# A decoder layer's up projection with the activations stationary: 512 weight columns moving, the result turned in squares and by transfers, the down projection in two parts

## The chip, the cores and the metric

The kernel runs on one core of a Trainium2 chip. The metric is the device time of one launch in microseconds (us), the median of three runs. The core has a matrix engine (TensorE, PE in the profile, with its weight loads on a row PEld), VectorE (DVE), ScalarE (ACT), GpSimd (POOL) and SyncE (SP, which here only issues DMA transfers). Each engine works through its own queue of instructions in order; semaphores tie the queues together.

## The reference

One layer of a decoder, 256 tokens of 2048 features, all in float32. The token mixers come first (an mLSTM and a forgetting attention, then an output projection); the change is in what follows, the gated MLP with a causal convolution of width 3 along the tokens:

```python
h = rms_norm(x, ffn_norm_g[i])            # (256, 2048)
u = h @ w_up[i]                           # (2048, 2 * 5632)
a, g = jnp.split(u, 2, axis=-1)           # (256, 5632) each
a = causal_dwconv(a, conv_w[i], conv_b[i])   # three taps along the tokens, one set per feature
x = x + (jax.nn.gelu(a, approximate=False) * g) @ w_down[i]
gate = jax.nn.sigmoid(rms_norm(x, ple_norm_g[i]) @ w_ple_gate[i])
x = x + gate * (p[i].astype(x.dtype) @ w_ple_proj[i])
```

## The kernel before, in words

**Precision.** Every float32 operand of a large product is split into a rounded part `hi` (type float32r, which PE takes at full rate) and a remainder `lo`; three products, hi by hi, hi by lo and lo by hi, are added up in PSUM. For the activations the parts lie side by side: a tile `[128 features, k, 512]` holds 256 tokens of hi and behind them 256 tokens of lo.

**The stream of weight blocks.** All weights are read once, in blocks of 128 x 1024 numbers (512 KB: two chunks of 128 rows by 512 columns), by `run_stream` (L205). For each block SP issues the load into a buffer `raw` (L218; four buffers, so four blocks ahead), ACT copies it to `hi` (L231), VectorE subtracts to get `lo` (L233), three blocks ahead of PE and in four buffers each, and then the block's function issues its matmuls. After each block `pull` takes some steps out of `side`, a list of generators with other work. The planner of the framework orders each engine's queue from this program text and a simulated run, so the text gives priorities and not the exact order.

**Two ways to multiply a block.** `token_group` (L242) keeps 128 tokens of the activations stationary and moves 512 weight columns past them: three matmuls (L261 to L263) for each of 2 chunks and 2 halves of the tokens, 12 matmuls of 512 columns a block; the result has tokens on partitions. It is used by the output projection (`catT`), by the down projection (`uT`) and by the gate after it (`x3T`). `wide_group` (L295), which only the up projection uses (`x2T`), keeps 128 x 128 of the weights stationary and moves activations: for each chunk and each of four groups of 128 columns, one matmul of 512 (weight hi past the tokens' hi and lo, L311) and one of 256 (weight lo past the tokens' hi, L312), 16 matmuls a block; the result has features on partitions, with 256 columns to be added to the other 256.

**The MLP.** The up projection runs over 11 quarters `q` of 512 features (a "quarter" of 4 x 128), each with 8 blocks for `a` and 8 for `g`: 176 blocks, 2816 matmuls. `up_a` and `up_g` add the two halves of a bank (`merge`, L724 and L725), multiply by the tokens' norm factors, which lie along the free dimension (`rb`, made by four small PE matmuls in `rstd_rows`, L165), apply the three taps with the features' scalars on the partitions (L738, L741), the GELU (L745), and the product with `g` (L759); `split_T` (L139, L140) writes the parts of the product into `uT`, which holds all 44 chunks of features. After all quarters, the down projection runs over four groups `c` of 512 output columns, each over 44 chunks of `uT` (22 blocks); `resid` adds its result to `xs` (L691) and transposes the sum on PE for the gate. All of this is issued in this order, on the same four buffers and queues; in this stage no generator is left in `side` and no DMA other than the weight loads is issued.

Of the kernel before, what the change touches and what calls it, by code (L numbers as in the profile page):

```python
# [9 lines left out]
F32 = mybir.dt.float32  # L10
F32R = mybir.dt.float32r
# [4 lines left out]
P = 128  # L16
S = 256
# [14 lines left out]

BLK = 1024
RAW, PARTS = 4, 4
AHEAD_DMA, AHEAD_SPLIT = 4, 3
PAD = 112


# [1 line left out]
def layer_kernel(  # L40
# [161 lines left out]
            except StopIteration:  # L202
                side.remove(job)

    def run_stream(blocks, pulls, ramp=False):  # L205

        nb = len(blocks)
        raws, parts = {}, {}
        split = 0
        for i in range(-AHEAD_DMA, nb):  # L210
            j = i + AHEAD_DMA
            if j < nb:
                src, _, _, load = blocks[j]
                if load is not None:
                    load()
                kb, n = src.shape[1], src.shape[2]
                raws[j] = wp.tile([P, BLK], F32, tag="raw", name=f"raw{j}", bufs=RAW)
                nc.sync.dma_start(out=raws[j][:, : kb * n].rearrange("p (k n) -> p k n", k=kb), in_=src)  # L218

            ahead = min(AHEAD_SPLIT, 1 + i // 2) if ramp else AHEAD_SPLIT  # L220
            while i >= -1 and split < min(nb, i + ahead + 1):
                j, split = split, split + 1
                src, _, prep, _ = blocks[j]
                if prep is not None:
                    prep()
                kb, n = src.shape[1], src.shape[2]
                w = kb * n
                raw = raws.pop(j)
                hi = wp.tile([P, BLK], F32R, tag="hi", name=f"hi{j}", bufs=PARTS)
                lo = wp.tile([P, BLK], F32R, tag="lo", name=f"lo{j}", bufs=PARTS)  # L230
                act.copy(hi[:, :w], raw[:, :w])  # L231
                last["hi"] = traced()
                dve.tensor_sub(lo[:, :w], raw[:, :w], f32(hi[:, :w]))  # L233
                parts[j] = [v[:, :w].rearrange("p (k n) -> p k n", k=kb) for v in (hi, lo)]
            if i >= 0:
                blocks[i][1](*parts.pop(i))
                pull(pulls)

    def wsrc(w, k0, kb, c0, n):
        return w[0, k0 * P : (k0 + kb) * P, c0 : c0 + n].rearrange("(k p) n -> p k n", p=P)  # L240

    def token_group(w, korder, actT, c0, n, finish, tag="mm", prep=None, load=None):  # L242

        st = {}
        blocks = []
        kb = min(BLK // n, 2 * len(korder))
        starts = [(k0, kb) for k0 in korder[:: kb // 2]]
        if load is not None:
            starts = [(0, 1), (1, 1)] + starts[1:]
        for bi, (k0, kb) in enumerate(starts):  # L250
            def fn(hi, lo, bi=bi, k0=k0):
                if bi == 0:
                    st["b"] = [bank(tag, f"tg{t}") for t in range(NT)]
                for t in range(NT):
                    o = st["b"][t][:, :n]
                    for i in range(hi.shape[1]):
                        a = actT()[:, k0 + i, :]
                        ah, al = a[:, t * P : (t + 1) * P], a[:, 256 + t * P : 256 + (t + 1) * P]
                        first = bi == 0 and i == 0
                        last = bi == len(starts) - 1 and i == hi.shape[1] - 1  # L260
                        pe.matmul(o, ah, hi[:, i, :], start=first, stop=False)  # L261
                        pe.matmul(o, ah, lo[:, i, :], start=False, stop=False)  # L262
                        pe.matmul(o, al, hi[:, i, :], start=False, stop=last)  # L263
                    if bi == len(starts) - 1:
                        finish(t, st["b"][t])
            pair = k0 % 2 == 0
            blocks.append((wsrc(w, k0, kb, c0, n), fn, pair and prep and (lambda k0=k0: prep(k0)) or None,
                           pair and load and (lambda k0=k0: load(k0)) or None))
        return blocks

    def feature_group(w, c0, actT, finish):
# [4 lines left out]
        for k0 in range(0, KD, 2):  # L276
            def fn(hi, lo, k0=k0):
                if k0 == 0:
                    st["b"] = [bank("mm", f"fg{j}").rearrange("p (j s) -> p j s", j=2) for j in range(2)]
                for j in range(4):  # L280
# [8 lines left out]
                        pe.matmul(o, lo[:, i, cols], a[:, 0:256], start=False, stop=last)  # L289
                    if k0 == KD - 2 and j % 2 == 1:  # L290
                        finish(j // 2, st["b"][j // 2])
            blocks.append((wsrc(w, k0, 2, c0, 512), fn, None, None))
        return blocks

    def wide_group(w, c0, actT, finish, tag):  # L295


        st = {}
        blocks = []
        for k0 in range(0, KD, 2):  # L300
            def fn(hi, lo, k0=k0):
                if k0 == 0:
                    st["b"] = [bank(tag, f"wg{j}") for j in range(4)]
                for j in range(4):
                    o = st["b"][j]
                    cols = slice(j * P, (j + 1) * P)
                    for i in range(2):
                        a = actT()[:, k0 + i, :]
                        first = k0 == 0 and i == 0
                        last = k0 == KD - 2 and i == 1  # L310
                        pe.matmul(o, hi[:, i, cols], a, start=first, stop=False)  # L311
                        pe.matmul(o[:, 256:512], lo[:, i, cols], a[:, 0:256], start=False, stop=last)  # L312
                    if k0 == KD - 2:
                        finish(j, o)
            blocks.append((wsrc(w, k0, 2, c0, 512), fn, None, None))
        return blocks

# [396 lines left out]


    with tc.tile_pool(name="ffn", bufs=1) as fp:
        uT = fp.tile([P, KF, 512], F32R, name="uT")
        rstd2 = rstd_of(ssq2, "ffn")
        rb = rstd_rows(rstd2, fp)
        rb2 = rb.unsqueeze(1).broadcast_to([P, 2, S])  # L720
        gl = {}

        def merge(dst, b):
            act.copy(dst, b[:, 256:512])  # L724
            dve.tensor_add(dst, b[:, 0:256], dst)  # L725

        def up_a(q):
            st = {}

            def f(jj, b):  # L730
                pair, j = divmod(jj, 2)
                if j == 0:
                    st["a"] = fp.tile([P, 2, S], F32, tag="a", name="a", bufs=2)
                    st["c"] = gl[q, pair] = fp.tile([P, 2, S], F32, tag="gl", name="c", bufs=3)
                a, c, k = st["a"], st["c"], 4 * q + jj
                merge(a[:, j], b)
                dve.tensor_mul(a[:, j], a[:, j], rb)
                act.activation(c[:, j], a[:, j], AF.Identity, scale=cT[:, 88 + k : 89 + k],  # L738
                               bias=cT[:, 132 + k : 133 + k])
                for d in (1, 2):  # L740
                    dve.scalar_tensor_tensor(out=c[:, j, d:S], in0=a[:, j, 0 : S - d],  # L741
                                             scalar=cT[:, 88 - 44 * d + k : 89 - 44 * d + k],
                                             in1=c[:, j, d:S], op0=ALU.mult, op1=ALU.add)
                if j == 1:
                    act.activation(c, c, AF.Gelu)  # L745
                    dve.tensor_mul(c, c, rb2)
            return f

        def up_g(q):
            st = {}  # L750

            def f(jj, b):
                pair, j = divmod(jj, 2)
                if j == 0:
                    st["u"] = fp.tile([P, 2, S], F32, tag="a", name="u", bufs=2)
                u, k = st["u"], 4 * q + 2 * pair
                merge(u[:, j], b)
                if j == 1:
                    dve.tensor_mul(u, u, gl.pop((q, pair)))  # L759
                    split_T(uT[:, k : k + 2, :], u)  # L760
            return f

        blocks = []
        x2 = aT["cur"]
        for q in range(KF // 4):
            blocks.extend(wide_group(w_up, q * 512, lambda: x2, up_a(q), "mm"))
            blocks.extend(wide_group(w_up, FF + q * 512, lambda: x2, up_g(q), "aux"))
        ssq3 = sm.tile([P, NT, 4], F32, name="ssq3")
        x3T = {}

# [2 lines left out]
                x3T["t"] = new_aT("x3T")  # L773
            return x3T["t"]

        for c in range(4):
            blocks.extend(token_group(w_down, list(range(0, KF, 2)), lambda: uT, c * 512, 512,
                                      resid(c, ssq3, get_x3T, g_ple)))


        r3, pj = {}, {}

# [3 lines left out]
        def gate_done(c0, n, last):  # L786
            def f(t, b):
                if "r" not in r3:
                    r3["r"] = rstd_of(ssq3, "ple")
                sg = fp.tile([P, 2, S], F32, tag="gl", name="sg", bufs=3).rearrange("p a b -> p (a b)")[:, :n]  # L790
                w = n // 2 if last and t == NT - 1 else n
                for c in range(0, n, w):
                    sc = sg[:, c : c + w]
# [7 lines left out]
        for c0, n in ((0, 512), (512, 512), (1024, 512), (1536, 256), (1792, 256)):  # L801
            blocks.extend(token_group(w_ple_proj, [0], lambda: pT, c0, n, proj_done, tag="aux"))
            blocks.extend(token_group(w_ple_gate, all_k, get_x3T, c0, n, gate_done(c0, n, c0 == 1792)))
        run_stream(blocks, 0)


# [28 lines left out]
```

## Time and profile before

| | |
|---|---|
| median of three runs | 1297.15 us (1296.51 to 1297.23) |
| span of the profiled execution | 1294.4 us |
| time around that span | 2.75 us, the median less the span |
| PE, PEld | 1288.3 us and 1123.9 us busy, 7060 instructions each |
| DVE, ACT, POOL | 754.9, 648.1 and 18.0 us busy |
| DMA | 238.69 MB, 184 GB/s |

A page of the profile gives, for one execution, the busy time of each engine, a strip of 40 slices (a digit is the busy share in tenths), the DMA queues, the chain of work that ended last (followed back from the last instruction, with shares of the span by line), and the costliest groups of instructions: line, engine, operation, result <- sources, shapes, count, then busy time and mean duration, then the idle time of that engine just before them and what ended it. L311 is line 311 of the kernel. Matmuls overlap, so the duration of one is longer than the distance from one to the next.

### The profile page before, as it was taken

What the parts mean: (1) busy time and instruction counts of PE and PEld (TensorE: products, weight loads), DVE (VectorE), ACT (ScalarE), POOL (GpSimd) and SP (SyncE); (2) the same over time, 40 slices, a digit from 0 to 9 for tenths busy, and PEclk for the clock granted to TensorE, in tenths of its full rate; (3) what the DMA queues carried; (4) which work ended last, traced back from release to release, by engine and by line L of the source; (5) the groups of instructions that cost most, each with busy time, mean ns of one, the idle gap of its engine ahead of it and who ended that gap; (6) DMA issues with size and microseconds to landing.
All of it is one profiled execution on the core that took longest, in us unless ns stands there. A gap on an engine that the chain in (4) does not pass through costs nothing.

```text
span 1294.4 us, 18152 instructions
## 1 busy us (share of the span) xinstructions
PE 1288.3 (100%) x7060; PEld 1123.9 (87%) x7060; DVE 754.9 (58%) x1008; ACT 648.1 (50%) x964; POOL 18.0 (1%) x33
## 2 busy tenths in 40 slices
PE   9999999999999999999999999999999999999998
PEld 7899999988888888888888888888888888888888
DVE  6455566644565565766676576667654545455554
ACT  7655545435554464555455454545543434444443
POOL 2000000000000000000000000000000000000000
PEclk9999999999999999999999999999999999999999
DMA  8577855546665666666666666666656665656663
GB/s 293 152 188 187 224 151 138 163 137 176 179 184 184 186 179 192 182 189 184 186 188 184 191 182 193 179 192 183 189 186 195 190 192 186 195 190 192 204 203 107
DMA packets 132039, 238.69 MB, mean 184 GB/s; under 512 B 7945, under 2 KB 28017, under 8 KB 131953
## 3 DMA queue, kind: packets, MB, share of 16 engines
q1 hardware_dynamic: 131072, 237.07, 61.7%
q8 instruction: 55, 0.90, 0.3%
q10 hardware_dynamic: 657, 0.43, 0.1%
q0 software_dynamic: 224, 0.03, 0.1%
q14 instruction: 31, 0.25, 0.1%
HBM read 235.40 MB, written 2.10 MB: 183 GB/s over the span
## 4 chain that ended last, share of the span: by engine, by line
PE 99%; DMA 0%; SPq 0%; DVE 0%; ACT 0%; issue 0%; DVEq 0%
PE wg L311 26%; PE tg L262 17%; PE tg L263 17%; PE tg L261 17%; PE wg L312 13%; PE fg L287 2%; PE fg L289 2%; PE fg L288 2%; PE xT L151 1%; PE mob L604 0%; DMA xs<-in_x_dram 0%; PE msc L578 0%; PE qkp L502 0%; PE sc L518 0%; PE ob L543 0%; PE rowb L489 0%
## 5 line engine op out<-in xcount | busy, mean ns | idle before, releaser
L233 DVE TENSOR_TENSOR lo<-raw,hi 128x1024 fp32r<-128x1024 f32 (+2 forms) x462 | 546.6, 1184 | 481.2 <-ACT hi L231 478.7
L231 ACT CAST hi<-raw 128x1024 fp32r<-128x1024 f32 (+2 forms) x462 | 470.4, 1018 | 567.9 <-PE tg L263 297.7
L311 PE MATMUL wg<-x2T,hi 128*128 128x512 f32 x1408 | 497.5, 399 | 0.0
L312 PE MATMUL wg<-x2T,lo 128*128 128x256 f32 x1408 | 395.4, 281 | 0.0
L311 PEld LDWEIGHTS wg<-x2T,hi 128*128 128x128 f32 x1408 | 264.5, 188 | 65.8
L312 PEld LDWEIGHTS wg<-x2T,lo 128*128 128x128 f32 x1408 | 266.0, 189 | 0.1
L261 PE MATMUL tg<-hi,uT 128*128 128x512 f32 x352 | 137.2, 390 | 0.0
L262 PE MATMUL tg<-lo,uT 128*128 128x512 f32 x352 | 137.0, 389 | 0.0
L263 PE MATMUL tg<-hi,uT 128*128 128x512 f32 x352 | 137.0, 389 | 0.0
L261 PE MATMUL tg<-hi,hT 128*128 128x512 f32 (+1 forms) x384 | 135.7, 358 | 0.0
L262 PE MATMUL tg<-lo,hT 128*128 128x512 f32 (+1 forms) x384 | 135.6, 356 | 0.0
L263 PE MATMUL tg<-hi,hT 128*128 128x512 f32 (+1 forms) x384 | 135.0, 356 | 0.0
L262 PEld LDWEIGHTS tg<-lo,hT 128*128 128x128 f32 x384 | 72.2, 188 | 7.5
L263 PEld LDWEIGHTS tg<-hi,hT 128*128 128x128 f32 x384 | 71.8, 188 | 7.2
L263 PEld LDWEIGHTS tg<-hi,uT 128*128 128x128 f32 x352 | 66.1, 188 | 13.7
L262 PEld LDWEIGHTS tg<-lo,uT 128*128 128x128 f32 x352 | 66.1, 188 | 13.6
L261 PEld LDWEIGHTS tg<-hi,uT 128*128 128x128 f32 x352 | 66.1, 188 | 13.6
L261 PEld LDWEIGHTS tg<-hi,hT 128*128 128x128 f32 x384 | 71.8, 188 | 6.9
L287 PE MATMUL fg<-hT,hi 128*128 128x256 f32 x256 | 74.7, 292 | 0.0
L289 PE MATMUL fg<-hT,lo 128*128 128x256 f32 x256 | 73.1, 285 | 0.0
L288 PE MATMUL fg<-hT,hi 128*128 128x256 f32 x256 | 72.8, 284 | 0.0
L262 PE MATMUL tg<-lo,x3T 128*128 128x512 f32 (+1 forms) x160 | 55.5, 347 | 0.0
(212 smaller groups left out, 1186.7 us busy)
## 6 DMA issues: line engine op xcount, KB each, us to landing
raw<-in_w_up_dram SPq DMA_DIRECT2D x176, 512.0 KB, 3.8
raw<-in_w_down_dram SPq DMA_DIRECT2D x88, 512.0 KB, 4.6
raw<-in_w_in_dram SPq DMA_DIRECT2D x79, 512.0 KB, 3.7
raw<-in_w_in_dram SPq DMA_DIRECT2D x48, 344.0 KB, 3.4
raw<-in_w_out_dram SPq DMA_DIRECT2D x32, 512.0 KB, 3.9
raw<-in_w_ple_gate_dram SPq DMA_DIRECT2D x32, 512.0 KB, 4.1
xs<-in_x_dram SPq DMA_DIRECT2D x8, 256.0 KB, 7.0
raw<-in_w_ple_proj_dram SPq DMA_DIRECT2D x3, 512.0 KB, 3.8
```

Source lines behind the costliest of these rows:

```text
L151: pe.transpose(bk[:, t * P : (t + 1) * P], xs[:, t, k * P : (k + 1) * P], ident)
L231: act.copy(hi[:, :w], raw[:, :w])
L233: dve.tensor_sub(lo[:, :w], raw[:, :w], f32(hi[:, :w]))
L261: pe.matmul(o, ah, hi[:, i, :], start=first, stop=False)
L262: pe.matmul(o, ah, lo[:, i, :], start=False, stop=False)
L263: pe.matmul(o, al, hi[:, i, :], start=False, stop=last)
L287: pe.matmul(o, hi[:, i, cols], a[:, 0:256], start=first, stop=False)
L288: pe.matmul(o, hi[:, i, cols], a[:, 256:512], start=False, stop=False)
L289: pe.matmul(o, lo[:, i, cols], a[:, 0:256], start=False, stop=last)
L311: pe.matmul(o, hi[:, i, cols], a, start=first, stop=False)
L312: pe.matmul(o[:, 256:512], lo[:, i, cols], a[:, 0:256], start=False, stop=last)
```

## The change

The up projection goes over to `token_group`; `wide_group`, `merge`, `up_a`, `up_g` and the use of `rstd_rows` here are removed. Its result now has tokens on partitions, and the taps need features there. So `up_evac` brings each bank out of PSUM on ACT with the tokens' norm factor as a scalar, and VectorE turns it in squares of 32 x 32, into a tile `sq`. After the last bank of a quarter a generator `ffn_job` is put into `side`: SP issues 16 transfers inside SBUF, each from 32 partitions to 32 others, which bring the squares into place in `Y`; then the taps are applied inside pieces of 32 tokens, and GpSimd makes what crosses the edges of the pieces (`halo`, `E`); then GELU, product and `split_T`. The tile `uT` keeps 24 chunks instead of 44, so the down projection is cut: after six quarters 20 chunks are multiplied for all four `c` and added to `xs` (`part_sum`), then the other five quarters follow, then the remaining 24 chunks. `run_stream` gets four more `raw` buffers in the second pool, eight loads ahead, and pulls two steps a block.

```diff
-AHEAD_DMA, AHEAD_SPLIT = 4, 3
+AHEAD_SPLIT = 3
+RAW_FFN = 4
+QF = 24
...
-    def run_stream(blocks, pulls, ramp=False):
+    def run_stream(blocks, pulls, ramp=False, more=None):
...
+        ring = RAW + (RAW_FFN if more else 0)
+        for i in range(-ring, nb):
+            j = i + ring
...
+                if j % ring < RAW:
+                    raws[j] = wp.tile([P, BLK], F32, tag="raw", name=f"raw{j}", bufs=RAW)
+                else:
+                    raws[j] = more.tile([P, BLK], F32, tag="raw", name=f"raw{j}", bufs=RAW_FFN)
...
-    def token_group(w, korder, actT, c0, n, finish, tag="mm", prep=None, load=None):
+    def token_group(w, korder, actT, c0, n, finish, tag="mm", prep=None, load=None, slots=10 ** 6):
...
-                        a = actT()[:, k0 + i, :]
+                        a = actT()[:, (k0 + i) % slots, :]
...
-    def wide_group(w, c0, actT, finish, tag):
...
-        uT = fp.tile([P, KF, 512], F32R, name="uT")
+        uT = fp.tile([P, QF, 512], F32R, name="uT")
         rstd2 = rstd_of(ssq2, "ffn")
-        rb = rstd_rows(rstd2, fp)
...
+        halo = [fp.tile([P, 4, NT, 4, 2], F32, name=f"halo{i}") for i in range(2)]
+        for h in halo:
+            pool.memset(h, 0.0)
+        sq = {}
+
+        def up_evac(q, ag):
+            def f(t, b):
+                if ag == 0 and t == 0:
+                    sq[q] = fp.tile([P, 2, 4, NT, 4, 32], F32, tag="sq", name="sq")
+                z = fp.tile([P, 512], F32, tag="z", name="z", bufs=3)
+                act.activation(z, b, AF.Copy, scale=rstd2[:, t : t + 1])
+                dve.transpose(sq[q][:, ag, :, t].rearrange("p j f r -> p f j r"),
+                              z.rearrange("p (f j c) -> p f j c", f=4, j=4))
+                if ag == 1 and t == NT - 1:
+                    side.append(ffn_job(q))
+            return f
+
+        def ffn_job(q):
+
+            T = sq.pop(q)
+            Y = fp.tile([P, 2, 4, NT, 4, 32], F32, tag="Y", name="Y")
+            for i in range(4):
+                for j in range(4):
+                    nc.sync.dma_start(out=Y[32 * j : 32 * j + 32, :, i], in_=T[32 * i : 32 * i + 32, :, j])
+                    if j % 2 == 1:
+                        yield
+            yield
+            yield
+            a, g = Y[:, 0], Y[:, 1]
+            taps = [cT[:, 44 * w + 4 * q : 44 * w + 4 * q + 4] for w in range(4)]
+            c = fp.tile([P, 4, NT, 4, 32], F32, tag="c", name="c")
+            H = halo[q % 2]
+            E = fp.tile([P, 4, NT, 4, 2], F32, tag="E", name="E", bufs=2)
+            e1 = fp.tile([P, 8, 4], F32, tag="e1", name="e1", bufs=2)
+            Hm, Em = (v.rearrange("p i t f e -> p (i t) f e") for v in (H, E))
+            pool.tensor_copy(H[:, 1:4].rearrange("p i t f e -> p (i t f) e"),
+                             a[:, 0:3, :, :, 30:32].rearrange("p i t f e -> p (i t f) e"))
+            pool.tensor_copy(H[:, 0, 1], a[:, 3, 0, :, 30:32])
+            pool.tensor_tensor(out=Em, in0=Hm, in1=taps[0].unsqueeze(1).unsqueeze(3).broadcast_to([P, 8, 4, 2]),
+                               op=ALU.mult)
+            pool.tensor_tensor(out=e1, in0=Hm[..., 1], in1=taps[1].unsqueeze(1).broadcast_to([P, 8, 4]), op=ALU.mult)
+            pool.tensor_tensor(out=Em[..., 0], in0=Em[..., 0], in1=e1, op=ALU.add)
+            am, cm = (v.rearrange("p i t f r -> p (i t) f r") for v in (a, c))
+            for f in range(4):
+                act.activation(cm[:, :, f], am[:, :, f], AF.Identity, scale=taps[2][:, f : f + 1],
+                               bias=taps[3][:, f : f + 1])
                 for d in (1, 2):
+                    dve.scalar_tensor_tensor(out=cm[:, :, f, d:32], in0=am[:, :, f, 0 : 32 - d],
+                                             scalar=taps[2 - d][:, f : f + 1], in1=cm[:, :, f, d:32],
+                                             op0=ALU.mult, op1=ALU.add)
+                if f % 2 == 1:
+                    yield
+            edge = c[..., 0:2].rearrange("p i t f e -> p (i t f) e")
+            dve.tensor_add(edge, edge, E.rearrange("p i t f e -> p (i t f) e"))
+            cf = c.rearrange("p i t f r -> p (i t f r)")
+            act.activation(cf, cf, AF.Gelu)
+            yield
+            u = a.rearrange("p i t f r -> p (i t f r)").rearrange("p (f t i r) -> p f t i r", f=4, t=NT, i=4)
+            for f in range(4):
+                dve.tensor_mul(u[:, f], c[:, :, :, f].rearrange("p i t r -> p t i r"),
+                               g[:, :, :, f].rearrange("p i t r -> p t i r"))
+            yield
+            k = 4 * q % QF
+            split_T(uT[:, k : k + 4, :], u.rearrange("p f t i r -> p f (t i r)"))
+            yield
...
+        def part_sum(c):
+            def f(t, b):
+                xc = xs[:, t, c * 512 : (c + 1) * 512]
+                dve.tensor_add(xc, b, xc)
+            return f
+
+        blocks = []
+        x2 = aT["cur"]
+
+        def up(q):
+            for ag in range(2):
+                blocks.extend(token_group(w_up, all_k, lambda: x2, ag * FF + q * 512, 512, up_evac(q, ag),
+                                          tag=("mm", "aux")[ag]))
+
+        def down(k0, k1, finish):
+            for c in range(4):
+                grp = token_group(w_down, list(range(k0, k1, 2)), lambda: uT, c * 512, 512, finish(c), slots=QF)
+                if c == 0:
+                    src, fn, _, _ = grp[-2]
+                    grp[-2] = (src, lambda hi, lo, fn=fn: (pull(10 ** 6), fn(hi, lo)), None, None)
+                blocks.extend(grp)
+
+        for q in range(6):
+            up(q)
+        down(0, 20, part_sum)
+        for q in range(6, KF // 4):
+            up(q)
+        down(20, KF, lambda c: resid(c, ssq3, get_x3T, g_ple))
...
-                sg = fp.tile([P, 2, S], F32, tag="gl", name="sg", bufs=3).rearrange("p a b -> p (a b)")[:, :n]
+                sg = fp.tile([P, 512], F32, tag="z", name="sg", bufs=3)[:, :n]
...
-        run_stream(blocks, 0)
+        run_stream(blocks, 2, more=fp)
```

More of the change, by code (lines that the diff above doesn't have):

```diff
@@ L209, in run_stream @@
         split = 0
-        for i in range(-AHEAD_DMA, nb):
-            j = i + AHEAD_DMA
+        ring = RAW + (RAW_FFN if more else 0)
+        for i in range(-ring, nb):
+            j = i + ring
             if j < nb:
@@ L216, in run_stream @@
                 kb, n = src.shape[1], src.shape[2]
-                raws[j] = wp.tile([P, BLK], F32, tag="raw", name=f"raw{j}", bufs=RAW)
+                if j % ring < RAW:
+                    raws[j] = wp.tile([P, BLK], F32, tag="raw", name=f"raw{j}", bufs=RAW)
+                else:
+                    raws[j] = more.tile([P, BLK], F32, tag="raw", name=f"raw{j}", bufs=RAW_FFN)
                 nc.sync.dma_start(out=raws[j][:, : kb * n].rearrange("p (k n) -> p k n", k=kb), in_=src)
@@ L291, in fn @@
                         finish(j // 2, st["b"][j // 2])
-            blocks.append((wsrc(w, k0, 2, c0, 512), fn, None, None))
-        return blocks
-    def wide_group(w, c0, actT, finish, tag):
[L298 to L314, printed above, removed]
             blocks.append((wsrc(w, k0, 2, c0, 512), fn, None, None))
@@ L716, in layer_kernel @@
     with tc.tile_pool(name="ffn", bufs=1) as fp:
-        uT = fp.tile([P, KF, 512], F32R, name="uT")
+        uT = fp.tile([P, QF, 512], F32R, name="uT")
         rstd2 = rstd_of(ssq2, "ffn")
-        rb = rstd_rows(rstd2, fp)
[L720 to L739, printed above, removed]
-                for d in (1, 2):
[L741 to L764, printed above, removed]
@@ L765, in layer_kernel @@
-        for q in range(KF // 4):
-            blocks.extend(wide_group(w_up, q * 512, lambda: x2, up_a(q), "mm"))
-            blocks.extend(wide_group(w_up, FF + q * 512, lambda: x2, up_g(q), "aux"))
+        halo = [fp.tile([P, 4, NT, 4, 2], F32, name=f"halo{i}") for i in range(2)]
[13 more added lines that the diff above has]
+            return f
@@ L774, in get_x3T @@
             return x3T["t"]
-        for c in range(4):
-            blocks.extend(token_group(w_down, list(range(0, KF, 2)), lambda: uT, c * 512, 512,
-                                      resid(c, ssq3, get_x3T, g_ple)))
+        def part_sum(c):
[22 more added lines that the diff above has]
+        down(20, KF, lambda c: resid(c, ssq3, get_x3T, g_ple))
         r3, pj = {}, {}
```

## Prediction

> **What bounds the kernel now.** I read the page first: the totals, the clock strip and the chain that ended last.
>
> ```profile
> span 1294.4 us, 18152 instructions
> ...
> PE 1288.3 (100%) x7060; PEld 1123.9 (87%) x7060; DVE 754.9 (58%) x1008; ACT 648.1 (50%) x964; POOL 18.0 (1%) x33
> ...
> PEclk9999999999999999999999999999999999999999
> ...
> PE 99%; DMA 0%; SPq 0%; DVE 0%; ACT 0%; issue 0%; DVEq 0%
> PE wg L311 26%; PE tg L262 17%; PE tg L263 17%; PE tg L261 17%; PE wg L312 13%; PE fg L287 2%; PE fg L289 2%; PE fg L288 2%; PE xT L151 1%; PE mob L604 0%; DMA xs<-in_x_dram 0%; PE msc L578 0%; PE qkp L502 0%; PE sc L518 0%; PE ob L543 0%; PE rowb L489 0%
> ```
>
> PE is busy in 100% of the span, the granted clock is full in every slice, and the chain is PE for 99%. So a change of this kernel is worth what it changes in PE's own time, plus any wait that it makes PE take. The up projection's two lines (L311, L312) carry 39% of the chain. The next view is the tile `wg`, which the up projection fills, with its matmuls and those who wait for them.
>
> ```profile
> L311 PE MATMUL wg<-x2T,hi x1408: 389/398/478, 449.0 to 947.4; 128*128 128x512 f32 x176
> ...
> L312 PE MATMUL wg<-x2T,lo x1408: 277/281/365, 449.3 to 947.6; 128*128 128x256 f32 x176
> ...
>   ACT hi L231: 204.0, 153
> ```
>
> The last row says that ACT's `hi` copy waits 204 us for these matmuls, while PE has no wait in this list: the splitting of weights runs ahead and is held back by PE, not the other way round. The windows view of most of the stage says the same by engine (columns: PE, PEld, DVE, ACT and POOL busy with counts, clock, DMA share, GB/s).
>
> ```profile
> 498.80:947.60 448.80, 448.80 (x2542) 389.19 (x2541) 297.49 (x416) 234.00 (x317) 0.00 (x0) 1.00 0.64 186
> ```
>
> PE is busy for all 448.80 us, DVE for 297.49 (66%), ACT for 234.00 (52%), DMA for 0.64 of it. There is no PE wait to remove; only the time per matmul can move.
>
> **The price per matmul, before and after.** L311 and L312 form 1408 pairs. The chain in order of time shows what else PE did inside these stages: transposes, in groups of eight.
>
> ```profile
> by line: PE wg L311 25.5%; PE tg L262 16.7%; PE tg L263 16.7%; PE tg L261 16.7%; PE wg L312 12.9%; PE fg L287 2.4%; PE fg L289 2.4%; PE fg L288 2.4%; PE xT L151 0.8%; PE mob L604 0.4%; DMA xs<-in_x_dram 0.3%; PE msc L578 0.3%; PE qkp L502 0
> ...
> 453.07 0.87 PE xT L151 x8
> 1012.55 0.87 PE xT L151 x8
> 1073.28 0.87 PE xT L151 x8
> 1134.01 0.87 PE xT L151 x8
> ```
>
> ```profile
> L165 PE MATMUL rstdb<-dg,ones x8: 270/273/275, 36.3 to 462.8; 128*128 128x128 f32 x8
> ```
>
> One transposing group (0.87 us, 0.109 us a matmul) lies in the up stage, and half of the eight `rstdb` matmuls, 0.4 us at the same 0.109. From the first to the last start of L311 are 498.4 us; less 1.3 that is 497.1 us for 1407 distances, 353.3 ns for a pair, 497.5 us for 1408 pairs. A pair moves 512 and 256 columns. What 512 columns cost in `token_group` form is shown by the down projection, which has the same instructions and shapes that the up projection is to get.
>
> ```profile
> L261 PE MATMUL tg<-hi,uT x352: 389/389/476, 947.8 to 1189.1; 128*128 128x512 f32 x176
> ...
> L263 PE MATMUL tg<-hi,uT x352: 389/389/393, 948.2 to 1189.6; 128*128 128x512 f32 x176
> ```
>
> From the first to the last start of L261 are 241.3 us, less three transposing groups in between (1012.55 to 1134.01) 238.7 us, for 351 x 3 = 1053 matmuls: 226.7 ns each. After the change there are 22 groups x 8 blocks x 12 = 2112 matmuls of 512 columns. That is the same number of columns, 1408 x 768 = 2112 x 512 = 1,081,344, in 704 fewer matmuls. So the new stage takes 2112 x 0.2267 = 478.8 us, 18.7 us less. A third form supports it: the mixers' `feature_group` moves 256 columns only.
>
> ```profile
> core 0: us, PE busy (x) PEld busy (x) DVE busy (x) ACT busy (x) POOL busy (x), PEclk, DMA share, GB/s
> 146.00:166.00 20.00, 20.00 (x168) 19.81 (x168) 12.08 (x23) 8.62 (x14) 0.00 (x0) 1.00 0.74 206
> ```
>
> Some 167 matmuls in 20.00 us are 120 ns each. From 120 for 256 and 226.7 for 512 follow 0.417 ns a column and 13 ns a matmul. 704 matmuls fewer at 13 ns are 9.4 us, half of the gain; the other half is that a pair takes 353.3 ns and not the 346.7 that its two lengths give alone. I have no cause for these 6.6 ns, but they belong to the alternation of the two lengths, which goes away.
>
> The Trainium skill (page "TensorE: Matmul & The Clock Gate", section "Back-to-back issue gap") gives a warm gap of the columns at 2.4 GHz plus 2.5 ns. By that the fixed part is small, the gain would be an estimated 704 x 2.5 ns = 1.8 us, and the change would hardly be worth measuring. The trace disagrees with this 2.5 ns here: 226.7 ns stands where the page's rule gives 215.8.
>
> **What else changes on PE.** The four `rstdb` matmuls go: 0.4 us less. The down projection stays at 88 blocks and 1056 matmuls; cut in two it has eight bank pairs rather than four, which changes no matmul. The gate at the end keeps its blocks.
>
> **What is added beside PE.** The terms of one quarter go by these rows (line, engine, operation; then busy time and mean ns).
>
> ```profile
> L738 ACT ACTIVATE c<-a,cT 128x256 f32<-128x256 f32 x44 | 24.1, 596 | 6.4 <-DVE a L737 6.4
> L724 ACT COPY a<-wg 128x256 f32<-128x256 f32 x44 | 16.2, 368 | 6.0 <-PE wg L312 6.0
> ...
> L745 ACT ACTIVATE c<-c 128x512 f32<-128x512 f32 x22 | 13.8, 627 | 0.3 <-DVE c L741 0.3
> ...
> L653 ACT ACTIVATE mv<-tg,rstd_mix 128x512 f32<-128x512 f32 x4 | 2.8, 690 | 1.9 <-PE tg L263 1.9
> ```
>
> ```profile
> L741 DVE SCALAR_TENSOR_TENSOR c<-a,cT,c 128x254 f32<-128x254 f32 x44 | 20.1, 478 | 0.0
> ...
> L725 DVE TENSOR_TENSOR a<-wg,a 128x256 f32<-128x256 f32 x44 | 16.5, 417 | 0.0
> ...
> L691 DVE TENSOR_TENSOR xs<-tg,xs 128x512 f32<-128x512 f32 x16 | 10.2, 682 | 0.0
> ```
>
> None of this can gain time, since PE waits for none of it now; the question is whether it stays hidden. ACT loses eight copies of 0.368 and gets four from PSUM with a scalar (0.69 each, L653); the taps (4 x 0.596, L738) and GELU (two of 0.627, now one of twice the length) stay: no more than before. VectorE loses 8 x 0.417 (L725) and all products with the norm factors, keeps the taps (8 x 0.478, L741), and gets four turns. The trace has no turn in squares. From below I set 0.417, a 128x256 operation with half the elements; from above four such, one for each 128 features, 1.7 us. I take 0.68, that of the 128x512 addition in L691, which reads and writes as many elements. The dearest case is 6.7 us a quarter; VectorE is idle in 34% of a quarter's 45.3 us (498.6 / 11), 15 us, so it is hidden in all of them, and up to some 3.8 us a turn. The eight `part_sum` additions (0.68 each) come once, beside PE.
>
> GpSimd gets five operations a quarter, on at most 64 numbers a partition. The trace has one of its kind only:
>
> ```profile
> L175 POOL TENSOR_TENSOR r_fk<-rs_v,neghalf 128x16 f32<-128x16 f32 x1 | 2.9, 2912 | 31.6 <-DVE rs_v L174 31.6
> ...
> L175 POOL TENSOR_TENSOR rstd_ffn<-rs_v,neghalf 128x2 f32<-128x2 f32 x1 | 0.7, 696 | 124.6 <-DVE rs_v L174 124.6
> ```
>
> These powers of 2 and 16 numbers bound the five at 3.5 and 14.5 us. I take 3.5: a copy, a product and a sum are no power. VectorE's edge addition waits for them.
>
> SP gets 16 transfers of 64 KB a quarter. The rows for its issue and the landing:
>
> ```profile
> L218 SPq DMA_DIRECT2D raw<-in_w_up_dram x176: 367/368/368, 431.6 to 927.9; - x176
> ...
> L218 SPq DMA_DIRECT2D raw<-in_w_ple_gate_dram x32: 367/368/739, 1176.0 to 1270.0; - x32
> ...
> DMA to landing us min/median/max: 2.4/3.9/7.2
> ```
>
> ```profile
> q1 hardware_dynamic: 131072, 237.07, 61.7%
> ```
>
> Issuing is 0.37 us whatever the size, so 16 more are 5.9 us a quarter beside 16 loads' 5.9. On the DMA engines, the first queue moved 131072 packets in 61.7% of 1294.4 us on 16 engines, 97 ns a packet. A quarter's 1 MB is 1024 pieces of 1 KB: by bytes 3.5 us, by packets 6.2 us of all engines, so DMA goes from 0.64 to at most 0.64 x 45.3 / 43.5 + 6.2 / 43.5 = 0.81. It stays under full.
>
> **The wait that the change adds.** In text order, ACT's taps stand behind the `hi` copy of the block eight after the quarter's last, and ahead of the copy of the ninth. If they wait for a transfer, so does that copy, and then VectorE and PE. How much room is there?
>
> ```profile
> 600.16 1.05 ACT L231 CAST hi<-raw 128x1024 fp32r<-128x1024 f32 x1 [1.74 <-PE wg L311]
> ...
> 601.24 1.22 DVE L233 TENSOR_TENSOR lo<-raw,hi 128x1024 fp32r<-128x1024 f32 x1 [1.56 <-ACT hi L231]
> ...
> 602.98 1.05 ACT L231 CAST hi<-raw 128x1024 fp32r<-128x1024 f32 x1 [1.77 <-PE wg L311]
> ```
>
> A `hi` copy starts when a block is through on PE, one every 2.8 us (2.72 after the change, 12 x 0.2267), and serves the block three later. Count from E, the end of the quarter's last block. Evacuation, turn and a split in front of them: the squares are ready by E + 3.7 (0.69 + 0.68 + 1.05 + 1.22; 1 us more if a turn takes 1.7). SP then issues 16 transfers and three loads, 19 x 0.367 = 7.0 us, and the last lands 3.9 us after its issue: E + 14.6. The copy of the ninth block may start at E + 13.6 (five blocks on), must be done with the subtraction by E + 21.8, so start by E + 19.5; the taps' four operations come before it, 2.4 us. So the transfers have until E + 17.1: 2.5 us to spare, and no time on PE. The edge addition stands before the subtraction of the tenth block, which must be through by E + 24.5: GpSimd has 8.7 us from the landing and takes 3.5. While SP waits for the squares, loads behind it wait too; with eight buffers they have some eight blocks (22 us) from issue to use and need 3.9, so that costs nothing. `uT` slots that are written again belong to chunks whose part of the down projection is long through. The last quarter's job has ten blocks (27 us) until its chunks are needed, and ends after about seven.
>
> **The sum.** 1294.4 - 18.7 - 0.4 = 1275.3 us of span; with the 2.75 us around it, which is the median 1297.15 less the span, **1278.0 us**.
>
> **Rivals.** *First, the transfers come late (slower).* The place is ACT's taps, L738's successor, in each quarter. Beyond E + 17.1 every microsecond stops PE once a quarter: 11 us. At 1.7 us late the gain is gone. For it: 2.5 us to spare is little, 7.2 us is the longest landing in the rows, and the trace has no transfer inside SBUF. At 7.2 instead of 3.9 PE would lose 0.8 x 11 = 9 us: 1287. If issuing cost 0.74 us (the longest row of L218) the last would land at E + 21.7, 4.6 late, 51 us: 1329. GpSimd at 14.5 us would be 5.8 late, 64 us: 1342. Against it: the longest issue is one of 32, a power is no copy, and the planner may bring `hi` copies ahead of waiting taps. *Second, the form brings nothing.* If in this stage time goes by columns alone, 353.3 / 768 = 0.460 ns each, 2112 x 512 of them take 497.4 us again and only `rstdb` is saved: 1296.7. If 512 columns keep what L311 has on the chain, 25.5% of 1294.4 over 1408 or 234.4 ns, the stage takes 495.1 us: 1294.3. Against it: the down projection's 226.7 has `hi` and `lo` moving just so, with the same splitting beside it. A cost of 2.5 ns a matmul, as the Trainium skill has it ("TensorE: Matmul & The Clock Gate", "Back-to-back issue gap"), would put the result near here, at an estimated 1294.9. *Third, small waits,* 0.2 to 1 us a quarter, from queues that the planner fills for times that differ from the chip's: 1281 to 1289.
>
> **Chances.** Forecast 0.72 (1275.5 to 1281; the lower end is a matmul of 225.5 ns, 0.5% less, 2.5 us in all). Third 0.12. First 0.10: 0.02 still faster, 0.01 same, 0.07 slower. Second 0.06: 0.01 faster, 0.05 same. 0.2% is 2.6 us, about what a measurement of this kernel can tell from no change. So faster by more than that 0.72 + 0.12 + 0.02 + 0.01 = 0.87, same 0.01 + 0.05 = 0.06, slower 0.07. The range goes to 1288, which takes in the forecast and nearly all of the third; the dear bounds of the first (1329, 1342) stay outside, with 0.18 in all.
>
> **What would show it.** Right: L261 to L263 with `x2T`, 704 of each, 226 to 227 ns apart; the stages up and down together (now 498.8 + 242) near 721 us with PE busy throughout; ACT's `hi` still waiting for PE; the turns near 0.7 us; the transfers landing in about 4 us. Wrong: PE rows with waits on ACT or DVE once a quarter some nine blocks after its end, ACT waiting on the DMA of `Y` for over 2 us, or a distance near 235 ns.

## The result and the profile after

The changed kernel takes **1278.34 us** (four runs, 1277.32 to 1279.7) against 1297.19 before (four runs): a ratio of 0.9853 with a 95% interval of 0.9839 to 0.9866, some 19 us less. The forecast was 1278.0. The profiled execution's span went from 1294.4 to 1275.4; its whole time is 1277.32, so 1.9 us lie around the span.

The page of the changed kernel, with the same lines as before:

```profile
span 1275.4 us, 16936 instructions
...
PE 1269.8 (100%) x6352; PEld 1088.8 (85%) x6352; DVE 732.3 (57%) x925; ACT 641.9 (50%) x898; POOL 33.2 (3%) x90
...
PEclk9999999999999999999999999999999999999999
...
PE 99%; DMA 0%; SPq 0%; DVE 0%; ACT 0%; issue 0%; DVEq 0%
PE tg L268 29%; PE tg L269 29%; PE tg L267 29%; PE fg L293 2%; PE fg L295 2%; PE fg L294 2%; PE xT L153 1%; PE mob L587 0%; DMA xs<-in_x_dram 0%; PE msc L561 0%; PE qkp L485 0%; PE sc L501 0%; PE ob L526 0%; PE rowb L472 0%; PE pt L520 0%; PE msc L564 0%
```

PE is still busy throughout, the clock is full, the chain is still PE. Only the lines in it are others: L267 to L269, the three matmuls of `token_group`, take what L311 and L312 had. The up projection's share of them, in the tile view of `x2T` (count, duration min/median/max, first and last start; then a waiter with total and times):

```profile
L267 PE MATMUL tg<-hi,x2T x704: 389/389/476, 449.2 to 1036.9; 128*128 128x512 f32 x176
...
L269 PE MATMUL tg<-hi,x2T x704: 389/389/393, 449.6 to 1037.4; 128*128 128x512 f32 x176
...
  ACT hi L237: 182.7, 114
```

And what the same matmuls do for the down projection, whose rows now straddle the second part of the up projection:

```profile
L267 PE MATMUL tg<-hi,uT x352: 389/389/476, 711.2 to 1170.1; 128*128 128x512 f32 x176
...
L269 PE MATMUL tg<-hi,uT x352: 389/389/393, 711.6 to 1170.6; 128*128 128x512 f32 x176
```

From the first start of L267 with `x2T` (449.2) to the first with `uT` (711.2) are 262.0 us; less one transposing group of 0.87, 261.1 us for six quarters of 192 matmuls: 226.7 ns each, as forecast. From the stage's start to the last down matmul (1170.6, and its 0.23) are 721.6 us; before, these two projections took 740.8 (449.0 to 1189.6, and 0.23). The 19.2 us between them are the whole change of the span, 19.0. ACT's `hi` copy still waits for PE; PE waits for nothing in these stages. The windows view of most of the first part:

```profile
498.80:709.00 210.20, 210.20 (x929) 174.07 (x928) 133.30 (x166) 112.54 (x127) 6.31 (x25) 1.00 0.67 219
```

The work that was added, in the tile views of `Y` and `sq` (SPq is SP's issue of a transfer):

```profile
L725 SPq DMA_DIRECT2D Y<-sq x176: 585/595/1703, 495.2 to 1049.2; - x176
...
  ACT c L746: 17.8, 11
...
DMA to landing us min/median/max: 2.0/2.0/3.7
```

```profile
L713 DVE STREAM_TRANSPOSE sq<-z x44: 701/705/712, 471.5 to 1038.5; 128x512 f32<-128x512 f32 x44
```

A turn takes 0.705 us, an issue 0.595, a landing 2.0. The end of the second quarter in order of time, ACT, VectorE and SP (start, duration, engine, line; in brackets the idle time before and what ended it):

```profile
537.30 0.69 ACT L712 ACTIVATE z<-tg,rstd_ffn 128x512 f32<-128x512 f32 x1 [0.67 <-PE tg L269]
...
538.03 0.71 DVE L713 STREAM_TRANSPOSE sq<-z 128x512 f32<-128x512 f32 x1 [0.51 <-ACT z L712]
...
538.80 10.71 SPq L725 DMA_DIRECT2D Y<-sq  x16
...
550.99 2.08 ACT L746 ACTIVATE c<-Y,cT 128x256 f32<-128x256 f32 x4 [1.75 <-DMA Y<-sq]
...
552.97 1.99 ACT L237 CAST hi<-raw 128x1024 fp32r<-128x1024 f32 x2
```

The quarter's last bank is through at 537.3. The 16 transfers are issued from 538.80 in one go, 10.71 us, and the taps wait for the last of them 1.75 us, until 550.99. That is 13.7 us behind the quarter's end, with the next `hi` copy at 15.7; it would have stopped PE from 19.5 on.

### The profile page after: what moved, and what is told of

Read it like the earlier page. It is cut to its first block, busy times and chain, and to the rows that moved or that the text cites. A ratio compares the mean times of both kernels' runs of the same rounds, so it can differ in the third digit from the quotient of the medians.

```text
span 1275.4 us, 16936 instructions
## 1 busy us (share of the span) xinstructions
PE 1269.8 (100%) x6352; PEld 1088.8 (85%) x6352; DVE 732.3 (57%) x925; ACT 641.9 (50%) x898; POOL 33.2 (3%) x90
## 4 chain that ended last, share of the span: by engine, by line
PE 99%; DMA 0%; SPq 0%; DVE 0%; ACT 0%; issue 0%; DVEq 0%
PE tg L268 29%; PE tg L269 29%; PE tg L267 29%; PE fg L293 2%; PE fg L295 2%; PE fg L294 2%; PE xT L153 1%; PE mob L587 0%; DMA xs<-in_x_dram 0%; PE msc L561 0%; PE qkp L485 0%; PE sc L501 0%; PE ob L526 0%; PE rowb L472 0%; PE pt L520 0%; PE msc L564 0%
## 5 line engine op out<-in xcount | busy, mean ns | idle before, releaser
L269 PE MATMUL tg<-hi,x2T 128*128 128x512 f32 x704 | 273.9, 389 | 0.0
L268 PE MATMUL tg<-lo,x2T 128*128 128x512 f32 x704 | 273.9, 389 | 0.0
L267 PE MATMUL tg<-hi,x2T 128*128 128x512 f32 x704 | 271.0, 389 | 0.0
L267 PEld LDWEIGHTS tg<-hi,x2T 128*128 128x128 f32 x704 | 132.1, 188 | 27.5
L268 PEld LDWEIGHTS tg<-lo,x2T 128*128 128x128 f32 x704 | 132.1, 188 | 27.4
L269 PEld LDWEIGHTS tg<-hi,x2T 128*128 128x128 f32 x704 | 132.1, 188 | 27.4
L267 PE MATMUL tg<-hi,uT 128*128 128x512 f32 x352 | 136.9, 390 | 0.0
L269 PE MATMUL tg<-hi,uT 128*128 128x512 f32 x352 | 136.8, 389 | 0.0
L267 PE MATMUL tg<-hi,hT 128*128 128x512 f32 (+1 forms) x384 | 135.7, 358 | 0.0
L269 PE MATMUL tg<-hi,hT 128*128 128x512 f32 (+1 forms) x384 | 135.0, 356 | 0.0
L269 PEld LDWEIGHTS tg<-hi,hT 128*128 128x128 f32 x384 | 71.8, 188 | 7.2
L269 PEld LDWEIGHTS tg<-hi,uT 128*128 128x128 f32 x352 | 66.1, 188 | 13.8
L268 PEld LDWEIGHTS tg<-lo,uT 128*128 128x128 f32 x352 | 66.1, 188 | 13.7
L267 PEld LDWEIGHTS tg<-hi,hT 128*128 128x128 f32 x384 | 71.8, 188 | 6.9
L267 PEld LDWEIGHTS tg<-hi,uT 128*128 128x128 f32 x352 | 66.1, 188 | 13.5
L293 PE MATMUL fg<-hT,hi 128*128 128x256 f32 x256 | 74.7, 292 | 0.0
```

The source lines that it names most:

```text
L293: pe.matmul(o, hi[:, i, cols], a[:, 0:256], start=first, stop=False)
```

## The experiments

All ratios are against the kernel before, timed beside each on the same chip.

**The form of the matmuls.** *Half width:* the changed kernel, each up matmul cut in two.

```diff
-                        pe.matmul(o, ah, hi[:, i, :], start=first, stop=False)
...
+                        w = cut or n
+                        for c in range(0, n, w):
+                            pe.matmul(o[:, c : c + w], ah, hi[:, i, c : c + w], start=first and c == 0, stop=False)
...
+                                          tag=("mm", "aux")[ag], cut=256))
```

> The changed kernel, with each matmul of the up projection cut in two of 256 columns: 4224 instead of 2112, same columns, same data path. The theory of 13 ns for every matmul (120 ns at 256) expects 4224 x 0.120 = 506.9 us instead of 478.8, 28 us more, about 1306. A rival with 2.5 ns a matmul expects 5 us more, 1284; columns alone expect 1278.

Measured 1307.29 us, ratio 1.0078 (1.0064 to 1.0092). That is 29 us over the changed kernel, for the same columns and the same data path, with 2112 matmuls more: 13.7 ns each, besides their columns. In the trace the halves start 120 ns apart. The Trainium skill ("TensorE: Matmul & The Clock Gate", "Back-to-back issue gap") has 2.5 ns for it; that would have been an estimated 5 us. The runs decide for 13, for this type of operand.

The 13 ns were fitted through two lengths, and the half-width run adds none, so a third one is worth reading: from 60 to 140 us the kernel before has nothing on PE but matmuls of 344 columns in `token_group` form. Its windows view there (PE alone):

```profile
60.00:140.00 80.00, 80.00 (x512) 1.00 0.72 191
```

511 distances in 80 us are 156.6 ns each; 0.417 ns x 344 columns and 13.3 ns are 156.7. So the three lengths lie on one line: a price by the column and a fixed price for each matmul. What inside PE takes the 13 ns is not shown by any run.

*Lengths grouped:* the kernel before, in each block first the eight long, then the eight short matmuls.

```diff
                 for j in range(4):
-                    o = st["b"][j]
...
+                        pe.matmul(st["b"][j], hi[:, i, cols], a, start=k0 == 0 and i == 0, stop=False)
+                for j in range(4):
...
                         pe.matmul(o[:, 256:512], lo[:, i, cols], a[:, 0:256], start=False, stop=last)
```

> The kernel before, with the sixteen matmuls of an up block put in another order: first the eight of 512 columns, then the eight of 256. Nothing else moves. The theory says that a pair's 353.3 ns are 226.7 + 120 plus 6.6 ns for the alternation of lengths: the stage shrinks by 1408 x 6.6 ns less the one change of length that is left in each half block, about 9 us, to 1288. The rival, that a column costs 0.460 ns in this stage in any order, expects 1297 as before.

Measured 1292.56, ratio 0.9960 (0.9946 to 0.9973): 5 us less, between the two (1288 and 1297). The chain in order of time of that kernel (L308 the long ones, L315 the short ones):

```profile
600.90 0.95 PE wg L315 x8
601.85 1.84 PE wg L308 x8
```

Eight long ones take 1.84 us, eight short ones 0.95, 2.79 us a block, where eight pairs took 2.83 and the plain sum of the lengths is 2.77. The starts in the trace show where the rest sits: behind the short ones the first five long ones take 228 to 236 ns, the last three 226 or 227. So a change of length costs some 20 ns a block here, and grouping saves only a part. This left the 6.6 ns a pair without a cause; the next run gave a lead by accident.

**The cut of the down projection.** *Down split only:* the kernel before, with nothing of the change but the two parts.

```diff
...
+        def down(k0, k1, finish):
+            for c in range(4):
+                blocks.extend(token_group(w_down, list(range(k0, k1, 2)), lambda: uT, c * 512, 512, finish(c)))
+
+        for q in range(6):
+            up(q)
+        down(0, 20, part_sum)
+        for q in range(6, KF // 4):
+            up(q)
+        down(20, KF, lambda c: resid(c, ssq3, get_x3T, g_ple))
```

> The kernel before, with only the down projection cut in two parts (20 chunks after six quarters, 24 at the end, eight part sums on VectorE); up projection, buffers and full uT as before. The theory puts this part at nothing: 1297.2 within 1 us. A rival in which the cut brings waits at its borders would show some microseconds more.

Measured 1292.61, ratio 0.9962 (0.9950 to 0.9975): 4.9 us *less*, where both theories had nothing or more. The windows view of L311 alone, 200 us of the up projection before the cut and 200 us behind it:

```profile
core 0: us, PE busy (x) PEld busy (x), PEclk, DMA share, GB/s
500.00:700.00 200.00, 200.00 (x567) 106.37 (x567) 1.00 0.60 187
840.00:1040.00 200.00, 200.00 (x578) 108.19 (x577) 1.00 0.62 192
```

The count in brackets at PE is of L311's matmuls: 567 in the first window, 578 in the second. Less one that reaches over the edge, a pair takes 353 ns before the cut and 346.6 behind it, with the same instructions and the same buffers. The 640 pairs behind the cut at 6.7 ns less make 4.3 of the 4.9 us. The starts in the trace repeat in steady cycles: 350, 361 and 349 ns from one L311 to the next in the windows up to the cut; soon behind it 343 (or 344) and 350. The old theory, that the alternation itself costs 6.6 ns, falls: alternating pairs run at 346.6, the plain sum of 226.7 and 120, or at 353.3.

**Two rhythms.** *One swap:* the kernel before, two matmuls exchanged at one place of 1408.

```diff
+                    swap = c0 == 512 and k0 == 4 and j == 1
...
                         pe.matmul(o, hi[:, i, cols], a, start=first, stop=False)
-                        pe.matmul(o[:, 256:512], lo[:, i, cols], a[:, 0:256], start=False, stop=last)
+                        if not swap:
+                            pe.matmul(o[:, 256:512], lo[:, i, cols], a[:, 0:256], start=False, stop=last)
+                    for i in range(2 if swap else 0):
+                        pe.matmul(o[:, 256:512], lo[:, i, cols], actT()[:, k0 + i, 0:256], start=False, stop=False)
```

> The kernel before with one pair of matmuls exchanged: in the second quarter, in one block, for one group of columns, both 512-column matmuls come ahead of both 256-column ones. All else stays. In the run with only the down projection cut, the pairs of the up projection took 353.3 ns up to the cut and 346.6 ns behind it, in steady cycles, though instructions and buffers were the same. New theory: an alternating sequence of 512 and 256 columns has two steady rhythms, and what comes before sets which one it falls into; then one exchange may tip it to 346.6 for the rest of the stage, 20 groups of 64 pairs by 6.6 ns, 8.5 us less, about 1289. If it falls back to 353.3 the theory is not refuted, but nothing is won: 1297. The old theory, that alternation itself costs 6.6 ns, expects 1297.

Measured 1288.58, ratio 0.9932 (0.9919 to 0.9944). The windows of its long matmuls, L312 in this kernel, behind the exchange:

```profile
520.00:720.00 200.00, 200.00 (x579) 108.16 (x578) 1.00 0.62 190
720.00:920.00 200.00, 200.00 (x578) 108.16 (x578) 1.00 0.61 190
```

From the exchange (at 505 us) to the end of the stage the pairs stay at 346.6 ns. One exchange is worth nearly half of what the whole change brought.

*Swap each group:* the same exchange in all 22 groups.

```diff
-                    swap = c0 == 512 and k0 == 4 and j == 1
+                    swap = k0 == 4 and j == 1
```

> As the run with one exchange, but the exchange is made once in each of the 22 groups of the up projection. If there are two rhythms, each exchange throws the dice again: groups at 346.6 and at 353.3 ns a pair, in steady cycles from each exchange on, and a time from 1288 to 1297. If the alternation itself costs 6.6 ns, every group stays at 353.3 and the time at 1297.

Measured 1296.23, ratio 0.9993 (0.9984 to 1.0002). The windows of its long matmuls (L312):

```profile
479.00:496.00 17.00, 16.93 (x50) 9.12 (x49) 1.00 0.63 189
500.00:700.00 200.00, 199.37 (x568) 105.80 (x567) 1.00 0.60 186
```

49 distances in 17 us are 347 ns, 567 in 200 us are 353. The second group's exchange (at 481.6 us by the starts) tips the pairs to 346.6, the third group's (503.8) tips them back, and the 19 later ones leave them at 353. So the exchange has no merit of its own: out of the slower rhythm it led to the faster one here once and in the run before, and 19 times it didn't. The starts show one difference. Ahead of each of those 19 the last distance was the long one of the cycle, 360 to 362 ns; ahead of the two that led to the faster rhythm it was one of 350. Whether this decides was not tried.

*No rstdb:* what had set the slow rhythm in the kernel before? In its trace the pairs behind the first transposing group step by 346 and 347 ns for a while, from 454 to 457.6 us. Then the first two of the four `rstdb` matmuls come in between (at 457.8), and a few pairs later the cycle is 350, 361 and 349.

```diff
-        rb = rstd_rows(rstd2, fp)
+        rb = fp.tile([P, S], F32, name="rb")
+        dve.tensor_scalar_mul(rb, ones[:, 0:1].broadcast_to([P, S]), rstd2[:, 0:1])
```

> The kernel before without the four small rstdb matmuls in the first quarter of the up projection; VectorE writes a stand-in for the norm factors instead, so each token gets the factor of another. All else stays. In the trace of before, the pairs behind the transposing group of the first quarter take 346.6 ns, until the first rstdb matmuls; behind these they take 353.3 for the rest of the stage. If these four set the rhythm, the stage stays at 346.6 and is about 9 us shorter, besides their own 0.4: 1288. If it is something else, only 0.4 us go: 1297.

Measured 1287.15, ratio 0.9925 (0.9911 to 0.9938), 9.7 us less. The windows of the long matmuls, L311 in both kernels, first in the kernel before, then in this one:

```profile
500.00:700.00 200.00, 200.00 (x567) 106.37 (x567) 1.00 0.64 187
720.00:920.00 200.00, 200.00 (x567) 106.35 (x566) 1.00 0.65 187
```

```profile
500.00:700.00 200.00, 200.00 (x578) 107.90 (x577) 1.00 0.61 190
720.00:920.00 200.00, 200.00 (x578) 107.87 (x577) 1.00 0.61 190
```

The counts of this run are those of the run with one swap: the stage keeps 346.6, here in steps of 346 and 347 ns, where one swap has 343 and 350. Four matmuls that took 0.4 us on the chain had cost 9 us more by what they left behind.

**The path beside PE.** *No transfers:* the squares are read where they lie, so features and tokens are mixed up; `sq` gets two buffers.

```diff
-                    sq[q] = fp.tile([P, 2, 4, NT, 4, 32], F32, tag="sq", name="sq")
+                    sq[q] = fp.tile([P, 2, 4, NT, 4, 32], F32, tag="sq", name="sq", bufs=2)
...
-            Y = fp.tile([P, 2, 4, NT, 4, 32], F32, tag="Y", name="Y")
-            for i in range(4):
-                for j in range(4):
-                    nc.sync.dma_start(out=Y[32 * j : 32 * j + 32, :, i], in_=T[32 * i : 32 * i + 32, :, j])
-                    if j % 2 == 1:
-                        yield
+            Y = T
+            for i in range(8):
+                yield
```

> The changed kernel without the 176 transfers that put the squares in place: the taps read the turned squares where they lie (so features and tokens are mixed up), from two buffers. All matmuls, turns and taps stay. The theory, in which the transfers are hidden whole, expects the changed kernel's 1278 within 1 us. The rival in which the transfers cost PE small waits expects the time that they cost to come back, 2 us or more.

Measured 1277.37, ratio 0.9845 (0.9832 to 0.9859), span 1276.0 against 1275.4: within a microsecond of the changed kernel. The 176 transfers are hidden.

*Four buffers:* without the added `raw` buffers.

```diff
-        run_stream(blocks, 2, more=fp)
+        run_stream(blocks, 2)
```

> The changed kernel with four raw buffers instead of eight. In its trace SP issues the 16 transfers of a quarter in one go, 10.7 us, with the loads behind them. With four buffers the load of the eighth block after the quarter's end would wait until 12.2 us after it, land at about 16.5, and must be there by 16.7. The theory expects next to nothing, 1278 to 1280. The rival, that the loads wait in the order of the text, between the transfers, and come 2 us late in each quarter, expects about 1300.

Measured 1280.26, ratio 0.9859 (0.9846 to 0.9873). ACT in the second quarter:

```profile
552.08 2.08 ACT L746 ACTIVATE c<-Y,cT 128x256 f32<-128x256 f32 x4 [4.88 <-DMA Y<-sq]
554.19 1.05 ACT L237 CAST hi<-raw 128x1024 fp32r<-128x1024 f32 x1
555.48 1.06 ACT L237 CAST hi<-raw 128x1024 fp32r<-128x1024 f32 x1 [0.23 <-DMA raw<-in_w_up_dram]
```

The planner has put the taps earlier; they wait 4.88 us for the transfers, and the second copy behind them starts 0.23 us late, with its load. PE waits for nothing in this stage; the span is 1276.5. The median is 1.9 us above the changed kernel's and 0.3 above the expected 1280, but the intervals of the ratios overlap, so no price of going without these buffers is shown.

*Double transfers:* 32 a quarter.

```diff
-                    nc.sync.dma_start(out=Y[32 * j : 32 * j + 32, :, i], in_=T[32 * i : 32 * i + 32, :, j])
+                    for h in range(2):
+                        nc.sync.dma_start(out=Y[32 * j : 32 * j + 32, h, i], in_=T[32 * i : 32 * i + 32, h, j])
```

> The changed kernel with each transfer cut in two (32 a quarter of 32 KB, same bytes). At 0.6 us of issue the last lands some 23 to 25 us after the quarter's end instead of 13.7. If the taps keep their place in ACT's queue (all that comes later than 17.1 us stops PE) this costs 6 to 8 us in each of 11 quarters: 1340 or more. If the planner puts the later hi copies ahead of the waiting taps, as the prediction held possible, it costs next to nothing: 1278 to 1285.

Measured 1279.40, ratio 0.9855 (0.9840 to 0.9870). SP in the second and third quarter:

```profile
540.73 10.24 SPq L726 DMA_DIRECT2D Y<-sq  x16
551.08 8.31 SPq L224 DMA_DIRECT2D raw<-in_w_up_dram  x8
560.86 1.78 SPq L726 DMA_DIRECT2D Y<-sq  x3
562.74 0.53 SPq L224 DMA_DIRECT2D raw<-in_w_up_dram  x1
563.31 1.14 SPq L726 DMA_DIRECT2D Y<-sq  x2
```

The planner leaves only 16 issues for the time after the quarter's end; the other 16, half of the bytes, go out between the loads while the quarter is still being multiplied, here from 560.86 for the third one. That these are the transfers of `a` follows from the program, as `a` is complete first; the view does not name them. PE waits for nothing. It also moved work on ACT, so this run does not show what a landing that is really late costs. That price was not measured.

**The same change once more.** *q turned* and *qk turned*: the mLSTM's queries, or queries and keys, which are the other products with the weights stationary, go to `token_group` and are turned in the same way; the second run also leaves out the four `rstdb` matmuls of the mixers, and GpSimd copies put its keys in order. The line for the queries, as the second run has it:

```diff
...
-            blocks.extend(feature_group(w_in, C_MQ + c * 512, lambda: hT, qk_group(mqT, c)))
+            add(C_MQ + c * 512, 512, q_turn(mqT, c))
...
```

> The changed kernel, and the same change made once more: the mLSTM's queries (two groups of 512 columns) are no longer multiplied with the weights stationary in 384 matmuls of 256 columns, but with the activations stationary in 192 of 512; ACT brings them out with the norm factor, VectorE turns them, 64 small transfers put them in place. The theory of 13.3 ns a matmul expects 384 x 0.120 - 192 x 0.2267 = 2.6 us less: 1275.7. If in this stage, where the attention's jobs share SP's four buffers, VectorE and PE, the transfers hold up the loads or the jobs, it expects 1278 or more.

Measured 1277.20, ratio 0.9839 (0.9825 to 0.9852).

> [...] The theory expects 5.1 + 0.4 us less than the changed kernel: 1272.8. Waits in the jobs that share the two small buffers used for turning would take some of it back.

Measured 1276.75, ratio 0.9840 (0.9827 to 0.9854), span 1273.8. Both are a microsecond or two below the changed kernel; the intervals overlap, so they are not told apart, and the expected 1275.7 and 1272.8 were missed. In the profiled executions the mixers, from the first matmul with `hT` to the first with `catT`, take 350.6 us in the changed kernel, 350.0 and 348.6 in these two: 0.7 and 2.0 us less, where 2.6 and 5.5 were expected. So the shortfall lies in the mixers themselves; what makes it is open. The attention's short matmuls come in between there every few microseconds, which the up projection does not have, and the sum of 226.7 a matmul took no account of that.

## Why the prediction was right, and where its reasons were not

*The time per matmul* was read from the down projection and carried over: 226.7 ns forecast, 226.7 measured; 18.7 + 0.4 us of gain forecast, 19.0 in the span. The second rival (time by columns alone, or nearly) is out, by the new rows and by the half-width run.

*The parts of that gain* were half right. That 13 ns a matmul make 9.4 us was a two-point fit and is confirmed: the 344-column matmuls lie on the same line, and the changed kernel is 10 us below the run with one swap and 9 below that without `rstdb`, both of which have the old form in the good rhythm. The other 9 us were put down to "the alternation of the two lengths, which goes away". That step failed. Pairs can alternate without loss, at 346.6 ns; the kernel before had been thrown into the slower of two rhythms, at 353.3. The sum held because a measured pair of 353.3 went into it and not the reason.

*The `rstdb` matmuls* were costed at their own 0.4 us. In the kernel before they cost 9.7, as the run without them shows. In the sum this is not an error, since the 9 us are in the pairs; but as the price of an edit "0.4" was wrong, and a version that took only these four away would have been forecast as no change.

*The down projection's two parts* at nothing: right for the changed kernel, whose matmuls are all of one length. In the kernel before the cut was worth 4.9 us, most of it again by the rhythm.

*The hidden path* was right in its sum and wrong in three terms, which cancelled; that the sum came so close is luck. The squares were ready 1.5 us behind the quarter's end, not 3.7, because no split came in between. An issue took 0.595 us and not "0.37 us whatever the size": 0.367 was the price of loads from HBM only. So 16 issues with no load among them took 10.7 us, where 19 were put at 7.0. A landing took 2.0 and not 3.9. The last transfer was there at 13.7 us, where 14.6 was forecast. The turn was 0.705 (0.68 taken). GpSimd's five operations took 0.19 to 0.36 us each on average, 1.4 in all, less than the lower bound of 3.5. DMA's share is 0.67, under the bound of 0.81.

*The first rival* (late transfers) did not come. In the second quarter it had 3.4 us to spare where 2.5 was forecast (the taps of the eleven quarters start 13.2 to 14.3 us behind the end, so 2.8 to 3.9 are left), and the runs with four buffers and with double transfers show that the planner finds room. *Small waits* did not come either.

*Around the span* the forecast added 2.75 us, a median less the span of one profiled execution. Taken the same way it is now 1278.34 - 1275.4 = 2.94. Only 1.9 of that lie around the span; the other 1.0 is there because the profiled execution was the shortest of four.

## What to carry to other kernels

On a kernel that PE bounds, price a change of form by the distance between starts in a stage of the same kernel that already has that form, not by a rule for the columns: it takes in the fixed cost of each matmul, here 13 ns. When two stages should run at the sum of their parts and one doesn't, look at the starts for a steady cycle, and try a trivial change of order before a large rebuild: one exchanged pair gave nearly half of what this change gave. A long path of turning and transfers costs nothing as long as its end is ahead of the point at which it stops the next split; that point can be worked out from the queue order, though no run here shows what a later end costs.

## What the runs showed of the hardware that was not expected

A steady sequence of a 512-column and a 256-column matmul in float32r ran at one of two mean distances on PE, 346.6 or 353.3 ns a pair, at full granted clock and with nothing waited for. A few small matmuls in between, another stage in between, or one exchange moved it from one to the other, and in five runs it then stayed for 200 us and more. What inside PE holds the slower one wasn't found.

Matmuls of 256, 344 and 512 columns in float32r started 120, 156.6 and 226.7 ns apart: 0.417 ns a column and 13 ns for each matmul.

An SP issue of a transfer inside SBUF took 0.595 us where a load from HBM took 0.367, though it moved an eighth of the bytes.
